# Five of eight row pairs by seven products in one up-projection block of each MLP, with the pairs in another order

## The chip, the cores and the metric

The kernel runs on one core of one Trainium2 chip. The metric is the device time of one execution in microseconds (us); three executions of the kernel before gave 1924.02, 1923.25 and 1924.7 us, so the median is 1924.02 us. The engines are named as in the profile: PE is the matmul engine (PEld its weight load), DVE the vector engine, ACT the scalar engine, POOL and SP the two others; SP issues the weight loads from memory.

## The reference

Two layers work on 256 tokens of width 2048, in float32. Layer 0 mixes tokens by a convolution module, layer 1 by latent attention. Each layer ends with the MLP that the change touches:

```python
def sq_relu_mlp(h, w1, w2):
    return jnp.square(jax.nn.relu(h @ w1)) @ w2
# per layer: x = x + mixer(rms_norm(x));  x = x + sq_relu_mlp(rms_norm(x), w1, w2)
# h: 256 x 2048, w1: 2048 x 8192, w2: 8192 x 2048
```

## The kernel before

**Float32 in three matmuls.** Every operand is split into a high part (rounded to the matmul's format, by an ACT copy) and a low part (the rest, by a DVE subtraction). A product of two operands is then three matmuls: high by high, low by high, high by low (`mm3`, lines 209 to 211). So each 1 MB piece of weights costs ACT copies and DVE subtractions before PE can use it. Pieces come through three `raw` buffers, and their parts through six `hi` and six `lo` buffers.

**The MLP's stages.** `mlp` works in two halves of the 8192 columns (`hf` 0 and 1). In a half, `UP_PLAN` lists the up-projection's blocks. Blocks 4, 5, 6 and 7 hold 512 columns each, with the weights standing in the array and the tokens moving (lines 812 and 813); results are evicted from the four `acc` banks by ACT and DVE (L829, L830, L832), squared, and split again (L715). Entries 0 and 2 are blocks of 1024 columns, with the tokens standing and the weights moving (`up_block`): these are the standing-input blocks. The order is block 4, block 5, standing-input block 0, block 6, standing-input block 2, block 7; then the down-projection of the half.

**A standing-input block.** Its 2048 input rows are eight pairs of 2 x 128 rows. For a pair, the two token tiles and the two column halves make eight products of 128x128 by 128x512, 24 matmuls (`Sums.plain`); the results gather in the four banks of the two `pair` tiles. `Sums.mixed` does the same with seven products, 21 matmuls, from sums and differences of the inputs and of the weights; it adds into the `pair` banks and into the four `acc` banks (u1, u6, u7, u5). For that, `mixed_weights` makes seven weight forms of a pair: four ACT copies, four DVE subtractions for low parts (L524, L525) and three DVE sums on `raw` (L532, L533, L534), against two copies and two subtractions of a plain pair (L176, L180). The input forms come once per half from `up_forms`, called at the (block, step) places of `UP_FORMS`; each call makes those of two pairs. `up_copies` rounds the inputs that plain pairs use. After the last seven-product pair, `Sums.parts` copies the `acc` banks out on ACT (L619) and combines them on DVE (L620 to L623).

Before, pairs 2, 3, 4 and 5 go by seven products (`UP_MIXED`), and the pairs run in the order 0, 2, 1, 3, 6, 4, 5, 7 (`UP_ORDER`) in all blocks.

**What sets the order.** The tile framework schedules the instructions of each engine in lists that are fixed when the program is built; an engine runs its list in order. In layer 0 the tables of the rotary embedding for layer 1 are made by DVE and ACT in block 5 of the second half (`beside`, small operations on `v` tiles, L1469 to L1513). Two `v` buffers serve all of this.

Of the kernel before, what the change touches and what calls it, by code (L numbers as in the profile page):

```python
# [45 lines left out]
HEAD, TAIL = (2, 1), 2  # L46
UP_PLAN, UP_ORDER, UP_MIXED = (4, 5, 0, 6, 2, 7), (0, 2, 1, 3, 6, 4, 5, 7), (2, 3, 4, 5)
UP_FORMS = ({(1, 1): 0, (1, 3): 1}, {(0, 2): 0, (1, 1): 1})
UP_COPIES = ({(1, 0): 0, (1, 2): 3}, {(1, 0): 0, (1, 2): 3})


# [31 lines left out]
def trunk_kernel(  # L83
# [59 lines left out]
    def nm(s):  # L143
        uid[0] += 1
        return f"{s}_{uid[0]}"
# [506 lines left out]
    def mlp(layer, ssq, next_gain, finish=None, before=None, beside=None, after_up=None):  # L652

        with ExitStack() as cx:
# [9 lines left out]
            def v_tile():  # L664
                rooms.clear()
                return mp.tile([P, 4, S], F32, tag="v", name=nm("v"), bufs=2)
# [10 lines left out]
                    nc.tensor.transpose(o[:, t * P : (t + 1) * P], r[:, t : t + 1].broadcast_to([P, P]), ident)  # L677
                nc.scalar.activation(r_row, o[:, :S], AF.Copy)

            def up_forms(i, fs):  # L680

                v, x = v_tile(), xt[UP_MIXED[2 * i] // 2].bitcast(F32)
                nc.vector.tensor_tensor(v, x[:, :, :S], x[:, :, S:], op=ALU.add)
                v = by_pairs(v)
                mixed_sums(*(v[:, :, j, :] for j in range(4)))
                h, l = (f[i][:, :, 3:, :] for f in fs)
                nc.scalar.activation(h, v, AF.Copy)
                nc.vector.tensor_tensor(l, v, h.bitcast(F32), op=ALU.subtract)
                x = x.rearrange("p (q k) n -> p q k n", q=2)
                for c, f in enumerate(fs):  # L690
                    nc.scalar.activation(f[i][:, :, 0, :], x[:, :, 0, c * S : c * S + P], AF.Copy)
                    nc.scalar.activation(
                        f[i][:, :, 1:3, :], x[:, :, 1, c * S : (c + 1) * S].rearrange("p q (t n) -> p q t n", t=T), AF.Copy
                    )

            def up_form(p, fs):

                i = UP_MIXED.index(p)

                def form(j):  # L700
                    return tuple(f[i // 2][:, i % 2, j, :] for f in fs)

                return form

# [27 lines left out]
            def up_block(hf, g, fs, copies):  # L732

                n = (hf * nkh + 4 * g) // 4
                sums = Sums(n, False, True)
                left = [p for p in UP_ORDER if p in UP_MIXED]

                def at_kt(c):
                    def at(k, t):
                        ts = slice(t * P, (t + 1) * P)  # L740
                        return copies[k // 4][c][:, k % 4, ts] if k // 4 in copies else (xh, xl)[c](k)[:, ts]
                    return at

                for p in UP_ORDER:
                    if p in UP_MIXED:
                        left.remove(p)
                        sums.mixed(mlp_w1[layer], 2 * p, up_form(p, fs), not left)
                        continue
                    end = p == UP_ORDER[-1]
                    if end:  # L750
                        zs = [v_tile().rearrange("p k n -> p (k n)") for _ in range(T)]
                        sums.parts(*(z[:, c * NB : (c + 1) * NB] for z in zs for c in range(2)))
                    sums.plain(mlp_w1[layer], 2 * p, at_kt(0), at_kt(1), 2 * p, end)
                for t, z in enumerate(zs):
                    o = z.rearrange("p (c n) -> p c n", c=2)
                    nc.vector.tensor_tensor(o, sums.pairs[t], o, op=ALU.add)
                    nc.scalar.activation(z, z, AF.Relu, scale=r_cols[0][:, t : t + 1])

                def turned():
                    pts = [a.rearrange("p b (k t n) -> p (b k) t n", t=T, n=P) for a in sums.pairs]  # L760
                    for c in range(2):
                        for f in range(4):
                            for t in range(T):
                                at = c * NB + f * P
                                nc.tensor.transpose(pts[c][:, f, t, :], zs[t][:, at : at + P], ident)  # L765
                    for c in range(2):
                        place(g + c)
                        v = v_tile()
                        nc.scalar.activation(v, pts[c].rearrange("p f t n -> p f (t n)"), AF.Square)
                        activations(g + c, v)  # L770

                return [turned]

            r_cols, late = [], []
            for hf in range(HALVES):
# [5 lines left out]
                fs = [[mp.tile([P, 2, 7, P], F32R, tag=f"s{c}", name=nm(f"f{c}"), bufs=N_MIXED) for _ in range(2)] for c in "hl"]  # L781
                copied = {
                    n: [mp.tile([P, 4, S], F32R, tag=f"g{c}", name=nm(f"x{c}"), bufs=ng - N_MIXED) for c in "hl"]
                    for n in UP_COPIES[hf].values()
                }
                for nth, g in enumerate(UP_PLAN):
                    if g in mixed:
                        late = up_block(hf, g, fs, {n: a for n, a in copied.items() if nth < 3 or n > 0})
                        continue
                    if nth == 0:  # L790
                        ends = [pair_tile() for _ in range(2)]
# [5 lines left out]
                    for u in range(KC // 4):  # L797
# [15 lines left out]
                                nc.tensor.matmul(ps[b][:, :S], wl[:, bs], xh(k), start=False, stop=k == KC - 1)  # L813
                        step(6)
                        if (nth, u) in UP_FORMS[hf]:
                            up_forms(UP_FORMS[hf][nth, u], fs)
                        if (nth, u) in UP_COPIES[hf]:
                            up_copies(UP_COPIES[hf][nth, u])
                        if late and u > 0:
# [1270 lines left out]
```

## Time and profile before

| what | value |
|---|---|
| median of three executions | 1924.02 us (1923.25 to 1924.7) |
| the profiled execution | 1923.38 us, its span 1921.6 us, granted PE clock 0.999 |
| PE busy | 1909.4 us (99%) |
| DVE busy | 1696.6 us (88%) |
| ACT busy | 1201.3 us (63%) |
| first standing-input block of layer 0's second half, PE | 683.01 to 723.96 us |
| the same in layer 1 | 1619.09 to 1659.90 us |

The span runs from the first to the last instruction; the execution's time has 1.8 us around it. A timeline row gives the start, the time, the engine, the line, the operation with what it writes and reads, and its count; in brackets stands the idle time before it and what ended it. Matmuls overlap, so their spacing counts and not their 0.39 us.

### The profile page before, as it was taken

How to read it: one execution, taken by the hardware profiler on the slowest of the kernel's cores; microseconds unless marked ns; L12 is line 12 of the kernel's file. 1: busy time of each engine (PE TensorE's matmuls, PEld its weight loads, DVE VectorE, ACT ScalarE, POOL GpSimd, SP SyncE). 2: the span in 40 equal slices, each digit the busy share in tenths (PEclk: the TensorE clock that was granted, in tenths of full speed). 3: DMA queues.
4: the chain of work that ended last, by engine and by line, in shares of the span. 5: the costliest groups of instructions: out<-in, count | busy, mean ns of one | idle time of the engine just before them, and what ended most of it. 6: DMA issues, size and time to landing. Idle time of an engine off the chain costs nothing.

```text
span 1921.6 us, 27587 instructions
## 1 busy us (share of the span) xinstructions
PE 1909.4 (99%) x10245; PEld 1653.2 (86%) x10245; DVE 1696.6 (88%) x2407; ACT 1201.3 (63%) x1701; POOL 248.6 (13%) x208
## 2 busy tenths in 40 slices
PE   9999999999999999999999999999999999999998
PEld 9999888888888888888888998888888888888887
DVE  7999989999999899999976765898999988898898
ACT  5667756666655666665576665576665647666554
POOL 6999200000010100000001420000000010000000
PEclk9999999999999999999999999999999999999999
DMA  7766455556585855655656445556556775655774
GB/s 228 211 185 186 156 186 196 187 186 219 176 250 198 252 167 193 229 178 199 217 168 183 138 137 177 173 176 219 188 173 225 219 246 199 219 180 195 233 221 147
DMA packets 214039, 375.43 MB, mean 195 GB/s; under 512 B 16392, under 2 KB 107792, under 8 KB 213648
## 3 DMA queue, kind: packets, MB, share of 16 engines
q1 hardware_dynamic: 208256, 363.28, 57.4%
q0 software_dynamic: 4320, 7.87, 2.2%
q10 hardware_dynamic: 1328, 2.52, 0.4%
q8 instruction: 80, 1.31, 0.3%
q14 instruction: 55, 0.45, 0.1%
HBM read 363.68 MB, written 2.10 MB: 190 GB/s over the span
## 4 chain that ended last, share of the span: by engine, by line
PE 96%; DVE 2%; ACT 1%; issue 0%; DMA 0%; DVEq 0%; ACTq 0%
PE acc L209 11%; PE acc L211 11%; PE acc L210 11%; PE pair L211 10%; PE pair L210 10%; PE pair L209 10%; PE acc L812 9%; PE acc L972 8%; PE acc L813 5%; PE pair L812 3%; PE acc L1436 2%; PE pair L813 2%; DVE sum L1059 1%; PE pair L765 1%; PE acc L1713 0%
## 5 line engine op out<-in xcount | busy, mean ns | idle before, releaser
L176 ACT ACTIVATE hi<-raw 128x1024 fp32r<-128x1024 f32 (+2 forms) x510 | 509.9, 1030 | 149.1 <-DMA raw<-in_mlp_w 44.1
L180 DVE TENSOR_TENSOR lo<-raw,hi 128x1024 fp32r<-128x1024 f32 (+2 forms) x445 | 519.2, 1193 | 89.4 <-ACT hi L176 84.7
L524 ACT ACTIVATE hi<-raw 128x1024 fp32r<-128x1024 f32 x376 | 347.0, 948 | 316.0 <-DVE raw L532 199.1
L525 DVE TENSOR_TENSOR lo<-raw,hi 128x1024 fp32r<-128x1024 f32 x376 | 400.2, 1088 | 26.9 <-ACT hi L524 21.0
L812 PE MATMUL acc<-xt,hi 128*128 128x512 f32 x768 | 268.0, 391 | 0.0
L813 PE MATMUL acc<-xt,lo 128*128 128x256 f32 x768 | 216.5, 282 | 0.0
L972 PE MATMUL acc<-xt,hi 128*128 128x256 f32 x1024 | 180.2, 281 | 0.4 <-ACT xt L1239 0.3
L611 POOL DMA_DIRECT2D xs<-v x30 | 26.3, 932 | 1128.3 <-DVE lo L180 696.2
L812 PEld LDWEIGHTS acc<-xt,hi 128*128 128x128 f32 x768 | 144.2, 188 | 30.1
L1059 DVE SCALAR_TENSOR_TENSOR sum<-ub,w_dw,sum 128x256 f32<-128x256 f32 x409 | 164.4, 485 | 3.6 <-ACT sum L1029 3.0
L180 POOL TENSOR_TENSOR lo<-raw,hi 128x1024 fp32r<-128x1024 f32 x65 | 155.0, 2408 | 18.0 <-ACT hi L176 18.0
L972 PEld LDWEIGHTS acc<-xt,hi 128*128 128x128 f32 x1024 | 154.7, 188 | 1.2 <-ACT xt L1239 0.8
L813 PEld LDWEIGHTS acc<-xt,lo 128*128 128x128 f32 x768 | 145.1, 189 | 0.3
L972 PE MATMUL acc<-xt,lo 128*128 128x256 f32 x512 | 139.2, 279 | 0.0
L532 DVE TENSOR_TENSOR raw<-raw 128x1024 f32<-128x1024 f32 x94 | 114.8, 1221 | 0.4
L209 PE MATMUL acc<-hi,sh 128*128 128x512 f32 x289 | 112.6, 390 | 0.0
L211 PE MATMUL acc<-lo,sh 128*128 128x512 f32 x289 | 112.5, 389 | 0.0
L210 PE MATMUL pair<-hi,gl 128*128 128x512 f32 (+1 forms) x264 | 101.9, 386 | 0.0
L211 PE MATMUL pair<-lo,gh 128*128 128x512 f32 (+1 forms) x264 | 101.9, 386 | 0.0
L209 PE MATMUL pair<-hi,gh 128*128 128x512 f32 (+1 forms) x264 | 101.9, 386 | 0.0
L209 PE MATMUL acc<-hi,gh 128*128 128x512 f32 x252 | 98.1, 389 | 0.0
L211 PE MATMUL acc<-lo,gh 128*128 128x512 f32 x252 | 98.0, 389 | 0.0
(381 smaller groups left out, 4299.1 us busy)
## 6 DMA issues: line engine op xcount, KB each, us to landing
raw<-in_mlp_w SPq DMA_DIRECT2D x255, 1024.0 KB, 5.5
raw<-in_conv_w_pw SPq DMA_DIRECT2D x62, 512.0 KB, 5.1
raw<-in_conv_w_pw SPq DMA_DIRECT2D x16, 1024.0 KB, 4.9
raw<-in_mla_w_o SPq DMA_DIRECT2D x16, 1024.0 KB, 5.1
raw<-in_mla_w_kv_up SPq DMA_DIRECT2D x32, 256.0 KB, 4.0
xs<-v POOLq DMA_DIRECT2D x30, 256.0 KB, 7.3
raw<-in_mla_w_in SPq DMA_DIRECT2D x8, 576.0 KB, 4.3
raw<-in_mla_w_in SPq DMA_DIRECT2D x4, 1024.0 KB
```

What stands on the lines that cost most here:

```text
L176: nc.scalar.activation(hi, raw[:, js, :], AF.Copy)
L180: eng.tensor_tensor(lo, raw, hi.bitcast(F32), op=ALU.subtract)
L209: nc.tensor.matmul(ps, sh, mh, start=start, stop=False)
L210: nc.tensor.matmul(ps, sl, mh, start=False, stop=False)
L211: nc.tensor.matmul(ps, sh, ml, start=False, stop=stop)
L524: nc.scalar.activation(hi, src, AF.Copy)
L525: nc.vector.tensor_tensor(lo, src, hi.bitcast(F32), op=ALU.subtract)
L532: nc.vector.tensor_tensor(top, raw[:, :, NB:], top, op=ALU.subtract)
L812: nc.tensor.matmul(ps[b], wh[:, bs], xhl(k), start=k == 0, stop=False)
L813: nc.tensor.matmul(ps[b][:, :S], wl[:, bs], xh(k), start=False, stop=k == KC - 1)
L972: nc.tensor.matmul(pss[c][b][:, :S], w[i][:, bs], (xh, xl)[j](k), start=k == i + j == 0, stop=end and k == k0 + nk - 1 and (i, j) == terms ...
L1059: nc.vector.scalar_tensor_tensor(out=out, in0=ubs[c][:, w : w + S], scalar=tap(c, w), in1=base, op0=ALU.mult, op1=ALU.add)
```

## The change

In the first standing-input block of the second half of each MLP, so twice in the whole run, pair 6 goes by seven products as well, and the pairs run in the order 2, 0, 3, 4, 1, 5, 6, 7. In the place before, block 5 of that half, a third call of `up_forms` makes the input forms of pair 6 alone (half of the tile, `slice(0, 1)`). All other blocks are as before.

```diff
+UP_MORE, UP_MORE_AT, UP_MORE_ORDER = 6, {1: (1, 2)}, (2, 0, 3, 4, 1, 5, 6, 7)
...
-            def up_forms(i, fs):
-
-                v, x = v_tile(), xt[UP_MIXED[2 * i] // 2].bitcast(F32)
-                nc.vector.tensor_tensor(v, x[:, :, :S], x[:, :, S:], op=ALU.add)
-                v = by_pairs(v)
+            def up_forms(n, f2, qs=slice(0, 2)):
+
+                ks = slice(2 * qs.start, 2 * qs.stop)
+                v, x = v_tile(), xt[n].bitcast(F32)
+                nc.vector.tensor_tensor(v[:, ks], x[:, ks, :S], x[:, ks, S:], op=ALU.add)
+                v = by_pairs(v)[:, qs]
                 mixed_sums(*(v[:, :, j, :] for j in range(4)))
...
-                left = [p for p in UP_ORDER if p in UP_MIXED]
+                more = UP_MORE // 2 in fs
+                order, by_seven = (UP_MORE_ORDER, (*UP_MIXED, UP_MORE)) if more else (UP_ORDER, UP_MIXED)
+                left = [p for p in order if p in by_seven]
...
-                for p in UP_ORDER:
-                    if p in UP_MIXED:
+                for p in order:
+                    if p in by_seven:
                         left.remove(p)
                         sums.mixed(mlp_w1[layer], 2 * p, up_form(p, fs), not left)
                         continue
-                    end = p == UP_ORDER[-1]
+                    end = p == order[-1]
...
+                more = {UP_MORE // 2: form_tiles()} if hf in UP_MORE_AT else {}
...
                     if g in mixed:
-                        late = up_block(hf, g, fs, {n: a for n, a in copied.items() if nth < 3 or n > 0})
+                        late = up_block(hf, g, fs | more, {n: a for n, a in copied.items() if nth < 3 or n > 0})
+                        more = {}
                         continue
...
                         if (nth, u) in UP_FORMS[hf]:
-                            up_forms(UP_FORMS[hf][nth, u], fs)
+                            n = UP_MIXED[2 * UP_FORMS[hf][nth, u]] // 2
+                            up_forms(n, fs[n])
+                        if (nth, u) == UP_MORE_AT.get(hf):
+                            up_forms(UP_MORE // 2, more[UP_MORE // 2], slice(0, 1))
```

Eight lines are added ahead of it, so that L830 of before is L838 of the change, L524 is L525, and so on.

**PE at the block's first use of the `acc` banks, layer 0.** Names with `pair` and `acc` are banks; `hi` and `lo` are weight parts, `fh`, `fl` input forms of a seven-product pair, `xh`, `xl` plain inputs. Before, the first seven-product pair follows pair 0, whose last row stands at the top:

```order
L211 MATMUL pair_7056<-lo_7068,xh_6623 128x512
L209 MATMUL acc_7057<-hi_7097,fh_6619 128x512 [waits DVE_49]
L210 MATMUL acc_7057<-hi_7097,fl_6621 128x512
L211 MATMUL acc_7057<-lo_7098,fh_6619 128x512
L209 MATMUL pair_7055<-hi_7097,fh_6619 128x512
```

Now, the block's first matmuls follow block 5's last one at the top:

```order
L818 MATMUL acc_6825<-xt_99,lo_6987 128x256
L210 MATMUL pair_7069<-hi_7077,fh_6619 128x512 [waits Activation_49]
L211 MATMUL pair_7069<-hi_7077,fl_6620 128x512
L212 MATMUL pair_7069<-lo_7078,fh_6619 128x512 [waits DVE_49]
L210 MATMUL pair_7069<-hi_7081,fh_6619 128x512 [waits Activation_49]
L211 MATMUL pair_7069<-hi_7081,fl_6620 128x512
L212 MATMUL pair_7069<-lo_7082,fh_6619 128x512 [waits DVE_49]
L210 MATMUL acc_7071<-hi_7077,fh_6619 128x512 [waits DVE_49]
```

The `acc` bank that block 5 filled is taken again after 6 matmuls instead of after 24; the DVE wait of that row is for its eviction. In layer 1 it is taken after 2.

**DVE at that eviction, layer 0.** Rows of L1486 and L1494 belong to the rotary tables. Before:

```order
L525 TENSOR_TENSOR lo_7109<-raw_7095,hi_7108 128x1024 [waits PE_49,Activation_49]
L1486 SCALAR_TENSOR_TENSOR v_7008<-v_7008 128x64 [waits DVE_49]
L830 TENSOR_TENSOR v_7042<-acc_6820,v_7042 128x256 [waits Activation_49]
L1486 SCALAR_TENSOR_TENSOR v_7008<-v_7008 128x64 [waits DVE_49]
L830 TENSOR_TENSOR v_7042<-acc_6821,v_7042 128x256 [waits Activation_49]
```

Now:

```order
L526 TENSOR_TENSOR lo_7089<-raw_7075,hi_7088 128x1024 [waits PE_49,Activation_49]
L1494 SCALAR_TENSOR_TENSOR v_7022<-v_7022 128x64 [waits DVE_49]
L526 TENSOR_TENSOR lo_7093<-raw_7075,hi_7092 128x1024 [waits PE_49,Activation_49]
L1494 SCALAR_TENSOR_TENSOR v_7022<-v_7022 128x64 [waits DVE_49]
L181 TENSOR_TENSOR lo_7120<-raw_7117,hi_7119 128x1024 [waits DMAHW0_49,PE_49,Activation_49]
L1494 SCALAR_TENSOR_TENSOR v_7022<-v_7022 128x64 [waits DVE_49]
L838 TENSOR_TENSOR v_7056<-acc_6822,v_7056 128x256 [waits Activation_49]
```

The first eviction stood behind both subtractions of pair 0 and three of pair 2's four; now it stands behind all four of pair 2's and one of pair 0's.

**ACT at the last seven-product pair, layer 0.** `hi_7291` to `hi_7306` are pair 5's weight forms of before, `hi_7313` to `hi_7328` pair 6's of the change; `hi_7343` and `hi_7365` are the first half of pair 7. Before:

```order
L524 ACTIVATE hi_7295<-raw_7289 128x512 [waits PE_49,Activation_49]
L524 ACTIVATE hi_7302<-raw_7289 128x1024 [waits DVE_49,PE_49,Activation_49]
L524 ACTIVATE hi_7306<-raw_7289 128x1024 [waits DVE_49,PE_49,Activation_49]
L176 ACTIVATE hi_7343<-raw_7341 128x1024 [waits DMAHW6_49,PE_49,Activation_49]
L619 ACTIVATE v_7331<-acc_7057 128x512 [waits PE_49]
```

Now:

```order
L525 ACTIVATE hi_7317<-raw_7311 128x512 [waits PE_49,Activation_49]
L620 ACTIVATE v_7353<-acc_7071 128x512 [waits PE_49]
L525 ACTIVATE hi_7324<-raw_7311 128x1024 [waits DVE_49,Activation_49]
L525 ACTIVATE hi_7328<-raw_7311 128x1024 [waits DVE_49,Activation_49]
L177 ACTIVATE hi_7365<-raw_7363 128x1024 [waits DMAHW6_49,Activation_49]
```

The copy of the bank u1, which waits for PE's products of this same pair, moved ahead of two of the pair's weight copies.

More of the change, by code (lines that the diff above doesn't have):

```diff
@@ L780, in mlp @@
                 gs = {}
-                fs = [[mp.tile([P, 2, 7, P], F32R, tag=f"s{c}", name=nm(f"f{c}"), bufs=N_MIXED) for _ in range(2)] for c in "hl"]
+                form_tiles = lambda: [mp.tile([P, 2, 7, P], F32R, tag=f"s{c}", name=nm(f"f{c}"), bufs=N_MIXED) for c in "hl"]
+                fs = {p // 2: form_tiles() for p in UP_MIXED[::2]}
+                more = {UP_MORE // 2: form_tiles()} if hf in UP_MORE_AT else {}
                 copied = {
```

13 lines of the change are left out of this document (6 added, 7 removed).

## The prediction

> **What bounds the kernel now.** I read the page's busy times and chain of waits first, then PE's, DVE's and ACT's timelines around the two blocks that change.
>
> ```profile
> PE 1909.4 (99%) x10245; PEld 1653.2 (86%) x10245; DVE 1696.6 (88%) x2407; ACT 1201.3 (63%) x1701; POOL 248.6 (13%) x208
> PE 96%; DVE 2%; ACT 1%; issue 0%; DMA 0%; DVEq 0%; ACTq 0%
> ```
>
> PE sets the end, so a matmul less is time less, as long as PE's inputs come in time. The 88% of DVE is a mean; what counts is the block itself. PE in layer 0's block (its first matmul, first seven-product pair, second plain pair, pair 7, a late matmul, the next block):
>
> ```profile
> 683.01 0.39 PE L209 MATMUL pair<-hi,xh 128*128 128x512 f32 x1
> 688.46 0.39 PE L209 MATMUL acc<-hi,fh 128*128 128x512 f32 x1
> 693.22 0.39 PE L209 MATMUL pair<-hi,xh 128*128 128x512 f32 x1
> 718.38 0.39 PE L209 MATMUL pair<-hi,xh 128*128 128x512 f32 x1
> 719.52 0.50 PE L211 MATMUL pair<-lo,xh 128*128 128x512 f32 x1
> 723.96 0.40 PE L812 MATMUL acc<-xt,hi 128*128 128x512 f32 x1
> PEld pair L211 <- DVE lo L180: 0.3, 1, 0.3
> ```
>
> A plain pair lasts 688.46 - 683.01 = 5.45 us, a seven-product pair 693.22 - 688.46 = 4.76, so a matmul costs 0.227 us (not the 0.39 of its row). The row at 719.52 lasts 0.50 for 0.39, and the wait's row says why: a low part of pair 7 came late. DVE reaches the end of this block with no lead left. Its work for pairs 3 and 6 and the block's tail:
>
> ```profile
> 693.34 1.82 DVE L525 TENSOR_TENSOR lo<-raw,hi 128x1024 fp32r<-128x1024 f32 x2
> 695.08 1.22 DVE L532 TENSOR_TENSOR raw<-raw 128x1024 f32<-128x1024 f32 x1
> 697.66 2.50 DVE L525 TENSOR_TENSOR lo<-raw,hi 128x1024 fp32r<-128x1024 f32 x2
> 700.08 2.35 DVE L180 TENSOR_TENSOR lo<-raw,hi 128x1024 fp32r<-128x1024 f32 x2
> 702.35 1.82 DVE L525 TENSOR_TENSOR lo<-raw,hi 128x1024 fp32r<-128x1024 f32 x2
> 715.86 1.23 DVE L525 TENSOR_TENSOR lo<-raw,hi 128x1024 fp32r<-128x1024 f32 x1 [1.21 <-ACT hi L524]
> 717.00 3.60 DVE L180 TENSOR_TENSOR lo<-raw,hi 128x1024 fp32r<-128x1024 f32 x3
> ```
>
> A seven-product pair takes DVE 700.08 - 693.34 = 6.74 us, a plain one 2.27. Per seven-product pair DVE is 1.98 us slower than PE, and per plain pair 3.18 faster. Before, four and four: DVE 36.0, PE 40.8 us. Now five and three: DVE 40.5, PE 40.2. The lead inside the block is gone, and the evictions of block 5 come on top.
>
> **What is saved.** In each of the two blocks 24 matmuls become 21: 3 x 0.227 = 0.68 us, 1.36 in all. No load is added: pair 6's 1 MB piece is fetched either way.
>
> **What is added ahead of the block.** Input forms of pair 6: on DVE an addition and a subtraction of 512 and four sums of 128; on ACT copies of 512, two of 256 and two of 128. The nearest rows in layer 0:
>
> ```profile
> L691 ACT ACTIVATE fh<-xt x1: 402/402/402, 651.2 to 651.2; 128x256 fp32r<-128x256 f32 x1
> L692 ACT ACTIVATE fh<-xt x1: 616/616/616, 651.5 to 651.5; 128x512 fp32r<-128x512 f32 x1
> 671.27 1.22 DVE L688 TENSOR_TENSOR fl<-v,fh 128x1024 fp32r<-128x1024 f32 x1
> 675.64 1.22 DVE L180 TENSOR_TENSOR lo<-raw,hi 128x1024 fp32r<-128x1024 f32 x1
> 678.11 1.22 DVE L525 TENSOR_TENSOR lo<-raw,hi 128x1024 fp32r<-128x1024 f32 x1
> 681.25 0.22 DVE L1486 SCALAR_TENSOR_TENSOR v<-v 128x64 f32<-128x64 f32 x1
> 681.39 0.69 DVE L533 TENSOR_TENSOR raw<-raw 128x512 f32<-128x512 f32 x1
> 684.66 0.42 DVE L830 TENSOR_TENSOR v<-acc,v 128x256 f32<-128x256 f32 x1
> 685.13 0.42 DVE L830 TENSOR_TENSOR v<-acc,v 128x256 f32<-128x256 f32 x1
> ```
>
> An operation of 512 holds DVE 0.6 us (0.69 less an overlap of some 0.09); one of 128 lies between the 64-wide and the 256-wide row, 0.22 and 0.42 with their tails, 0.14 and 0.33 without. Together 2 x 0.6 + 4 x (0.14 to 0.33) = 1.8 to 2.5 us of DVE. Woven between the rotary rows, each of which waits for the one before, some of it costs nothing; I take 1.3, with 0.9 and 2.5 as ends.
>
> **The first stop, layer 0.** The block now begins with pair 2, and after 6 matmuls, at 683.01 + 6 x 0.227 = 684.37, PE wants the first `acc` bank, which block 5 has just filled. Before, pair 0 filled the `pair` banks first, and the bank was wanted only at 688.46; its eviction (684.66) was hidden by that pair. Where is the eviction now? Pair 0's two subtractions (675.64 to 678.11, 2.47 us) move behind pair 2's; one of them and pair 2's last subtraction now stand ahead of the eviction, each 1.14 with a rotary row of 0.13 (681.25 to 681.39 is 0.14): 684.66 - 2.47 + 2.54 + 1.3 = 686.0. It ends 0.42 later, so PE stops from 684.37 to 686.45: **2.1 us** (1.7 to 3.3). The other three banks follow 0.47 apart, and PE takes one per 0.68.
>
> **The later stops, layer 0.** PE's first two pairs end at 683.01 + 4.76 + 5.45 + 2.1 = 695.3. On DVE four evictions (1.9), the scaling L832 and the other half of pair 0 (2.5 with rotary rows) end at 690.4; pair 3 with L715 (1.14) inside takes till 698.5, pair 4 till 705.2, pair 1 till 707.5, pair 5 till 714.2, pair 6 till 721.0. ACT's high parts follow within a pair:
>
> ```profile
> 696.39 1.07 ACT L524 ACTIVATE hi<-raw 128x1024 fp32r<-128x1024 f32 x1 [2.94 <-DVE raw L532]
> 697.84 1.06 ACT L524 ACTIVATE hi<-raw 128x1024 fp32r<-128x1024 f32 x1 [0.38 <-DVE raw L534]
> 716.68 0.58 ACT L619 ACTIVATE v<-acc 128x512 f32<-128x512 f32 x1
> ```
>
> They end 4.1 and 5.6 us after DVE began the pair (693.34). PE wants the first 9 matmuls into a pair (2.04), the second 4 later (0.9).
> - Pair 3: PE 695.3 to 700.1, no stop.
> - Pair 4: wanted 702.1, there at 702.6; then wanted 703.5, there at 704.1. **1.1 us**; it ends 705.9.
> - Pair 1 to 711.4, pair 5 to 716.2, no stop.
> - Pair 6: ACT must first copy u1, the output of this pair's first product: 716.2 + 0.7 + 0.2 = 717.1, plus 0.5; so the weight copy ends at 718.7, wanted 718.2. **0.5 us**; it ends 721.4.
> - Pair 7: the low part of its second half needs 721.0 + 2 x 1.2 and ACT's two u copies (0.6 more), 724.0; wanted 10 matmuls in, 723.7. **0.3 us**; the block ends at 727.2.
>
> Against 723.96 that is +3.2: stops 4.0, less 0.68 saved, less the 0.1 of the stop at 719.52 that it replaces.
>
> **Layer 1.** No rotary rows here.
>
> ```profile
> 1619.09 0.39 PE L209 MATMUL pair<-hi,xh 128*128 128x512 f32 x1
> 1659.90 0.40 PE L812 MATMUL acc<-xt,hi 128*128 128x512 f32 x1
> 1609.51 3.50 DVE L180 TENSOR_TENSOR lo<-raw,hi 128x1024 fp32r<-128x1024 f32 x3 [1.62 <-ACT hi L176]
> 1612.92 1.22 DVE L525 TENSOR_TENSOR lo<-raw,hi 128x1024 fp32r<-128x1024 f32 x1
> 1618.72 1.09 DVE L830 TENSOR_TENSOR v<-acc,v 128x256 f32<-128x256 f32 x3
> ```
>
> DVE waited 1.62 us for ACT; ACT's new copies (0.52 + 2 x 0.31 + 2 x 0.2, about 1.6) lengthen that, so block 5's last subtraction starts near 1611.1 and pair 2's at 1612.25. Those end at 1619.0, one of pair 0 at 1620.1, the first eviction 1620.5. PE wants that bank after 2 matmuls, 1619.54: **1.0 us** (0.5 to 1.8). From there DVE's 6.74 per seven-product pair brings pair 6's low parts at 1652.9, wanted 1653.0, and pair 7's at 1657.1, wanted 1657.1: 0 to 0.7, I take **0.3**. Net +0.7 with rounding, 1.3 - 0.68.
>
> **The sum.** +3.2 and +0.7: +3.9 us. The span goes from 1921.6 to 1925.5, the profiled execution (1.8 around it) to 1927.3; the median of the runs lies 0.64 above that execution, so it becomes 1924.02 + 3.9 = **1927.9 us**, 0.2% slower.
>
> **The rivals.**
> - *DVE's lead is enough; not slower.* If pair 6's forms slip into waits and the eviction ends by 684.4, the order is harmless and the saving remains: 1924.0 - 1.36 = 1922.7, up to 1924.5 with stops of under 2 us. For it: DVE waits 1.62 us ahead of the block in layer 1. Against: the late row at 719.52, and 2.1 us to make up. Chance 0.2.
> - *Only the first stops.* If a seven-product pair costs DVE 6.4 (four of 1.14 and three of 0.6 with no wait between dependent rows) the later stops go: 2.1 + 1.0 - 1.36 - 0.1 = +1.6, 1925.6. Against: 6.74 in the quoted pair. Chance 0.12.
> - *A longer stop, and PE's clock falls.* At the upper end of the new DVE work the first stop is 3.3 us, 1.2 more.
>
> ```profile
> 1900.00:1921.00 21.00, 13.83 (x73) 11.76 (x71) 12.98 (x34) 5.36 (x12) 0.00 (x0) 0.95 0.28 101
> 953.00:983.00 30.00, 28.78 (x145) 24.15 (x144) 27.34 (x40) 17.61 (x31) 0.00 (x0) 1.00 0.46 142
> ```
>
> In the first stretch PE stood 7.2 us and its granted clock was 0.95, so 1.05 us of 21 were lost; in the second it stood 1.2 us and the clock stayed at 1.00. With such a loss: 3.9 + 1.2 + 1.05, 1930.2. The Trainium skill (TensorE: Matmul & The Clock Gate, What's actually happening) says the clock halves after an idle window of about 3.4 us; by that rule my 2.1 us cost no clock, and both rows agree. Chance 0.08.
>
> **How the numbers follow.** My forecast has 0.6, with its own range 1926.0 to 1929.6. A change within 0.2% (3.85 us) can't be told from none here, and 3.9 stands on that edge: half of the 0.6 is within it and half slower. With the clock's 0.08, slower has 0.38 to 0.4; within 0.2% has 0.3 + 0.12 + nearly all of the 0.2, less some spread: 0.57; faster by over 0.2% is beyond the whole saving, 0.03. The range of 8 in 10 is 1923.2 to 1930.4.
>
> **What would show it.** A wait of PE on L838 near 684 of about 2 us and near 1619.5 of about 1; waits on L525 in pair 4 and pair 6 in layer 0; the block 44.2 us long in layer 0 and 41.5 in layer 1, for 40.95 and 40.81. I am wrong if PE shows no wait on an eviction, or if the time is under 1924.

## The result and the profile after

The changed kernel took 1929.5 us as the median of seven executions (1928.36 to 1931.48), against 1924.02 before (seven executions, 1923.12 to 1924.7): a ratio of 1.0029, 95% interval 1.002 to 1.0039. So it is slower by 5.5 us, where the prediction said 3.9. The traced execution of the change took 1930.75 us, span 1929.0, so it lies in the upper part of the seven; the traces differ by 7.4 us.

The page of the changed kernel, its busy times and its chain of waits; then three rows of the table of what PE waited for (in all, times, longest):

```profile
PE 1909.6 (99%) x10239; PEld 1649.5 (86%) x10239; DVE 1707.6 (89%) x2429; ACT 1205.7 (63%) x1715; POOL 248.8 (13%) x208
PE 93%; DVE 4%; ACT 1%; issue 1%; DMA 1%; SPq 0%; DVEq 0%; ACTq 0%
```

```profile
PE acc L210 <- DVE v L838: 5.0, 2, 3.7
PE acc L212 <- DVE lo L526: 0.4, 1, 0.4
PE acc L210 <- ACT hi L525: 0.3, 1, 0.3
```

PE issues six matmuls fewer (10239 for 10245), as planned; two waits for an eviction (L838) are new. In the chain DVE has 4% for 2%. PE's timeline around the two blocks:

```profile
682.26 0.39 PE L210 MATMUL pair<-hi,fh 128*128 128x512 f32 x1
...
687.45 0.50 PE L210 MATMUL acc<-hi,fh 128*128 128x512 f32 x1 [3.65 <-DVE v L838]
...
689.09 0.63 PE L212 MATMUL acc<-lo,fh 128*128 128x512 f32 x1
689.52 0.63 PE L210 MATMUL acc<-hi,fh 128*128 128x512 f32 x1
689.95 0.63 PE L211 MATMUL acc<-hi,fl 128*128 128x512 f32 x1
...
692.58 0.39 PE L210 MATMUL pair<-hi,xh 128*128 128x512 f32 x1
...
720.24 0.50 PE L210 MATMUL acc<-hi,fh 128*128 128x512 f32 x1 [0.28 <-ACT hi L525]
...
728.92 0.40 PE L817 MATMUL acc<-xt,hi 128*128 128x512 f32 x1
...
1624.28 0.39 PE L210 MATMUL pair<-hi,fh 128*128 128x512 f32 x1
1626.22 0.50 PE L210 MATMUL acc<-hi,fh 128*128 128x512 f32 x1 [1.32 <-DVE v L838]
...
1658.92 0.50 PE L212 MATMUL acc<-lo,fh 128*128 128x512 f32 x1 [0.42 <-DVE lo L526]
...
1666.83 0.40 PE L817 MATMUL acc<-xt,hi 128*128 128x512 f32 x1
```

Layer 0's block is now 728.92 - 682.26 = 46.66 us long, for 40.95; layer 1's 1666.83 - 1624.28 = 42.55, for 40.81. Together +7.45, and the span grew by 7.4. (Elsewhere small shifts cancel: PE reaches the first block 0.75 us sooner, and the rest takes 0.7 longer.)

The first pair shows how. Six matmuls end at 682.26 + 6 x 0.227 = 683.62; the next begins at 687.45, so PE stood **3.83 us**. From 688 to 692 the matmuls are 0.43 us apart in place of 0.227. The first pair takes 692.58 - 682.26 = 10.32 us instead of 4.76: 5.56 lost, 3.83 by the stop and some 1.7 by the slow matmuls. The rest of the block lost 0.94 by late weights, 0.68 was saved, and 0.11 of lateness was there before: 5.56 + 0.94 - 0.68 - 0.11 = 5.71. In layer 1 two matmuls fit ahead: 1626.22 - 1624.28 - 0.45 = 1.49 us of stop, 0.11 right behind it, no slow matmuls, 0.80 later.

Busy time and granted clock in stretches of layer 0's block (span of the row, busy PE, PEld, DVE, ACT, POOL, granted clock, DMA share, GB/s):

```profile
682.00:688.00 6.00, 2.35 (x11) 1.65 (x10) 6.00 (x15) 5.62 (x9) 0.00 (x0) 1.00 0.31 85
688.00:692.00 4.00, 4.00 (x12) 3.13 (x11) 4.00 (x9) 2.70 (x4) 0.00 (x0) 0.57 0.50 207
692.00:729.00 37.00, 36.73 (x161) 29.41 (x160) 35.29 (x40) 23.13 (x30) 0.00 (x0) 1.00 0.57 188
```

The clock fell to 0.57 behind the stop. DVE is busy 6.00 of 6.00, then 4.00 of 4.00, then 35.29 of 37; its two waits in that last stretch, 0.68 us at 720.22 and 0.61 at 724.33, are for ACT's copies. So two readings of the loss are open: **the stop reading** (the new order meets the eviction, PE stands, the clock falls; DVE's load inside the block matters little) and **the chain reading** (DVE works with hardly a pause up to the block's last low part, and PE would have to wait for it somewhere, wherever the first stop falls).

### The profile page after: what moved, and what is told of

Same layout as the page of the kernel before. It is cut to its first block, busy times and chain, and to the rows that moved or that the text cites. A ratio compares the mean times of both kernels' runs of the same rounds, so it can differ in the third digit from the quotient of the medians.

```text
span 1929.0 us, 27619 instructions
## 1 busy us (share of the span) xinstructions
PE 1909.6 (99%) x10239; PEld 1649.5 (86%) x10239; DVE 1707.6 (89%) x2429; ACT 1205.7 (63%) x1715; POOL 248.8 (13%) x208
## 4 chain that ended last, share of the span: by engine, by line
PE 93%; DVE 4%; ACT 1%; issue 1%; DMA 1%; SPq 0%; DVEq 0%; ACTq 0%
PE acc L210 11%; PE acc L212 11%; PE acc L211 11%; PE pair L212 10%; PE pair L210 10%; PE pair L211 10%; PE acc L817 8%; PE acc L980 8%; PE acc L818 4%; PE pair L817 3%; PE acc L1444 2%; PE pair L818 1%; DVE sum L1067 1%; PE pair L767 1%; DVE lo L526 0%
## 5 line engine op out<-in xcount | busy, mean ns | idle before, releaser
L181 DVE TENSOR_TENSOR lo<-raw,hi 128x1024 fp32r<-128x1024 f32 (+2 forms) x441 | 513.8, 1191 | 89.0 <-ACT hi L177 84.0
L525 ACT ACTIVATE hi<-raw 128x1024 fp32r<-128x1024 f32 (+1 forms) x384 | 353.7, 947 | 317.4 <-DVE raw L533 205.0
L526 DVE TENSOR_TENSOR lo<-raw,hi 128x1024 fp32r<-128x1024 f32 (+1 forms) x384 | 408.3, 1087 | 27.0 <-ACT hi L525 19.7
```

The source lines that it names most:

```text
L181: eng.tensor_tensor(lo, raw, hi.bitcast(F32), op=ALU.subtract)
L525: nc.scalar.activation(hi, src, AF.Copy)
L526: nc.vector.tensor_tensor(lo, src, hi.bitcast(F32), op=ALU.subtract)
```

## The experiments

Edits are against the changed kernel. Block lengths are read from each run's timeline of PE, from the block's first matmul to the next block's.

| run | layer 0, us | layer 1, us | median, us | ratio to before, 95% |
|---|---|---|---|---|
| before | 40.95 | 40.81 | 1924.02 | |
| the change | 46.66 | 42.55 | 1929.5 | 1.0029 (1.002 to 1.0039) |
| order_alone | 46.08 | 42.32 | 1928.7 | 1.0025 (1.0015 to 1.0035) |
| order_bare | 43.51 | 41.04 | 1926.67 | 1.0015 (1.0005 to 1.0025) |
| forms_only | 43.44 | 40.81 | 1925.07 | 1.0007 (0.9998 to 1.0017) |
| fill_stop | 47.36 | 42.36 | 1931.49 | 1.0037 (1.0024 to 1.005) |
| fill_order | 44.36 | 45.12 | 1929.85 | 1.0028 (1.0017 to 1.0039) |
| plain_first | 45.56 | 43.52 | 1930.1 | 1.0032 (1.002 to 1.0044) |
| l1_only | 41.63 | 42.41 | 1925.42 | 1.001 (1.000 to 1.002) |
| rope_last | 43.78 | 42.79 | 1930.76 | 1.0037 (1.0023 to 1.005) |
| rope_early | 48.31 | 43.49 | 1935.94 | 1.0062 (1.0047 to 1.0077) |
| forms_early | 49.47 | 48.1 | 1938.31 | 1.0072 (1.0055 to 1.0088) |
| pool_01 | 51.0 | 45.9 | 1938.84 | 1.0077 (1.006 to 1.0093) |

(Lengths with one decimal are counted from the end of block 5's last matmul, since the block's own first one waited.)

### The order without the fifth pair

```diff
-UP_MORE, UP_MORE_AT, UP_MORE_ORDER = 6, {1: (1, 2)}, (2, 0, 3, 4, 1, 5, 6, 7)
+UP_MORE, UP_MORE_AT, UP_MORE_ORDER = 6, {1: (1, 2)}, (2, 0, 3, 1, 6, 4, 5, 7)
...
-                order, by_seven = (UP_MORE_ORDER, (*UP_MIXED, UP_MORE)) if more else (UP_ORDER, UP_MIXED)
+                order, by_seven = (UP_MORE_ORDER, UP_MIXED) if more else (UP_ORDER, UP_MIXED)
```

Pair 6 goes plainly; its forms are still made, and nobody reads them.

> The new order's beginning without the fifth pair: four pairs by seven products in the order 2, 0, 3, 1, 6, 4, 5, 7; the input forms of pair 6 are still made, but not used. So DVE has 4.5 us less in each block than in the change, and the eviction stands where the change has it. Theory A: the first stop is as in the change (3.8 us and 1.6), with the fall of the clock in layer 0: median 1928 to 1931. Theory B: the first stop is there, but the late stops go, since DVE catches up; blocks of 43 to 45 and 41.5 to 42.5 us, median 1926 to 1929. If the fifth pair is the whole cause: no more than 1925.

Order and forms without the fifth pair cost nearly all: 46.08 and 42.32 us, 1928.7 (1929.5 for the whole change). The stop and the slow clock are there, and nothing is late after them:

```profile
687.31 0.56 PE L210 MATMUL acc<-hi,fh 128*128 128x512 f32 x1 [3.38 <-DVE v L838]
```

```profile
688.00:692.00 4.00, 4.00 (x13) 3.08 (x13) 4.00 (x9) 2.70 (x4) 0.00 (x0) 0.62 0.45 185
692.00:729.00 37.00, 37.00 (x165) 30.68 (x164) 33.69 (x37) 23.01 (x29) 0.00 (x0) 1.00 0.63 215
```

PE is busy 37.00 of 37 behind the stop, and DVE has 3.3 us to spare. With four pairs the stop reading holds. The fifth pair adds just 0.58 and 0.23 us to the blocks: in layer 0 its own saving of 0.68 is eaten by 0.94 of late weights, and a little more.

### The order and the forms, each by itself

For order_bare the call that makes pair 6's forms is left out of order_alone as well. For forms_only the forms are made and not read, and pairs and order are those of before.

```diff
 # order_bare, on top of order_alone
-                more = {UP_MORE // 2: form_tiles()} if hf in UP_MORE_AT else {}
+                more = {UP_MORE // 2: None} if hf in UP_MORE_AT else {}
...
-                        if (nth, u) == UP_MORE_AT.get(hf):
+                        if False:
 # forms_only
-UP_MORE, UP_MORE_AT, UP_MORE_ORDER = 6, {1: (1, 2)}, (2, 0, 3, 4, 1, 5, 6, 7)
+UP_MORE, UP_MORE_AT, UP_MORE_ORDER = 6, {1: (1, 2)}, (0, 2, 1, 3, 6, 4, 5, 7)
...
-                order, by_seven = (UP_MORE_ORDER, (*UP_MIXED, UP_MORE)) if more else (UP_ORDER, UP_MIXED)
+                order, by_seven = (UP_MORE_ORDER, UP_MIXED) if more else (UP_ORDER, UP_MIXED)
```

> Four pairs by seven products as before, in the new kind of order (a seven-product pair first: 2, 0, 3, 1, 6, 4, 5, 7), and no input forms of pair 6 at all. Against the run of the order alone it leaves out only the making of the unused forms. If those forms' place on DVE is what makes the first stop long (some 2 us of DVE work put in ahead of the eviction of L838), the stop of layer 0 falls from 3.8 to 1.6-2.2 us, the clock stays at 1.00, the block of layer 0 is 42.5-43.2 us long and that of layer 1 40.9-41.2, and the time is 1925.8-1926.5. If the order is enough for the stop and the forms lie in time that nobody waits for, the stop stays over 3 us, the clock falls again, the blocks stay near 46 and 42.3 and the time near 1928.7.

> The order of before (0, 2, 1, 3, 6, 4, 5, 7) and four pairs by seven products; the new input forms of pair 6 are made where the change makes them, but nothing reads them. If DVE's lead in a block that begins with a plain pair hides them (DVE 36.0 us of work against PE's 40.8 in the block), no wait appears, the blocks stay at 40.9-41.2 and the time at 1923.7-1924.4. If two microseconds of DVE work there cost as such, the block of layer 0 is 42-43 us long and the time 1925-1926.

In layer 0 the traced blocks grew by about the same: 43.51 (+2.56) for the order, 43.44 (+2.49) for the forms; together (order_alone) +5.13. In layer 1 the order costs 0.23, the forms nothing, and both together 1.51. PE's rows of order_bare, then of forms_only:

```profile
682.26 0.39 PE L210 MATMUL pair<-hi,fh 128*128 128x512 f32 x1
685.06 0.50 PE L210 MATMUL acc<-hi,fh 128*128 128x512 f32 x1 [2.40 <-DVE v L838]
```

```profile
717.74 0.50 PE L210 MATMUL pair<-hi,fh 128*128 128x512 f32 x1 [0.58 <-ACT hi L525]
719.00 0.51 PE L212 MATMUL pair<-lo,fh 128*128 128x512 f32 x1 [0.53 <-DVE lo L526]
725.99 0.40 PE L817 MATMUL acc<-xt,hi 128*128 128x512 f32 x1
```

Without the forms PE gets the first bank 2.4 us sooner (685.06 for 687.45): 0.84 of it because DVE started sooner in this execution (the row that waits for the stores, shown further down for the change, starts at 645.03 and not 645.87), the other 1.5 are what the forms take of DVE. The clock stayed at full. But here the program's list puts one matmul and not six ahead of the first `acc` bank, so PE still stands 685.06 - 682.49 = 2.57 us. (The traced execution is the fastest of this run's ten, 1924.99 us of up to 1930.84, so these blocks need not be those of the median.)

forms_only went against what I expected of it. DVE work that nothing reads, in the old order and with an eviction that nobody waits for, made weights late in pairs 5 and 7 of layer 0. The block began 0.46 us sooner than before and ended 2.03 later, 725.99 for 723.96: DVE was 0.58 later already ahead of the forms (L715 at 669.61 for 669.03), and the forms, with the places that the lists gave the rest of DVE's work, add the other 1.45. So even before, DVE reached the end of that block with nothing in hand, and in layer 1 it had this much to spare. This speaks for the chain reading. (The times of the runs rose by only 1.1 us, an amount that a measurement here hardly tells from none.)

### The stop filled with useless matmuls

32 transposes into a bank that is overwritten later stand behind the first six matmuls in layer 0's block; they add no result.

```diff
...
+            elif self.fill:
+                work = [work[i] for i in (4, 5, 0, 1, 2, 6, 3)]
-            for ps, i, (wh, wl) in work:
+            for at, (ps, i, (wh, wl)) in enumerate(work):
+                if self.fill and at == 2:
+                    for r in range(self.fill):
+                        nc.tensor.transpose(self.e[1][1][:, r % 4 * P : (r % 4 + 1) * P], ident, ident)
+                    self.fill = 0
...
+                sums.fill = 32 if more and layer == 0 else 0
```

> The changed kernel, with 32 transposes of 128 columns (3.5 us) put into PE's queue in layer 0's block between the products into the pair banks and the first product into an acc bank, so that PE works through most of its stop; their results are overwritten. Nothing else moves. Theory A (the loss is PE's first stop and the fall of its clock after it): the clock stays at 1.00 after the stop, the twelve matmuls at 0.43 us go back to 0.227, and the block is 1.7 us shorter than 46.7, the median near 1927.8. Theory B (DVE works without a pause from block 5 to the block's last low part, and its end sets the block's end): the clock stays up too, but the time is the same within 0.5 us (1929.0 to 1929.9); PE waits longer for weight parts in pairs 4, 6 and 7 instead.

> The run of the order alone (four pairs, unused forms made, stop of 3.8 us and slow clock in layer 0) with 32 transposes of no use in that stop, to keep TensorE busy. Here DVE has no fifth pair to work on. If the slower matmuls behind the stop are a loss by themselves where DVE isn't the bound, the block of layer 0 falls from 46.1 to 44.2-44.5 us, the clock row there stays at 1.00, and the time is 1926.7-1927.3. If DVE's chain sets the end here as well, the block stays at 45.7-46.3 with new waits on the low parts or high parts of weights (L526, L525) behind the start, and the time at 1928.3-1929.

In layer 0's block the clock stayed at full in both. Row of the stretch for fill_stop and its new waits, then the row for fill_order:

```profile
688.00:692.00 4.00, 4.00 (x19) 3.31 (x18) 4.00 (x9) 2.07 (x4) 0.00 (x0) 1.00 0.48 196
```

```profile
PE acc L212 <- DVE lo L526: 1.3, 3, 0.6
PE pair L210 <- ACT hi L525: 0.6, 1, 0.6
PE pair L212 <- DVE lo L526: 0.5, 1, 0.5
```

```profile
688.00:692.00 4.00, 4.00 (x19) 3.30 (x18) 4.00 (x11) 2.07 (x3) 0.00 (x0) 1.00 0.56 224
```

With four pairs the block of layer 0 became 1.72 us shorter (44.36 for 46.08): there the slow clock cost what its matmuls show. With five pairs it didn't become shorter at all (47.36 for 46.66): PE came to the later pairs sooner and waited there for DVE's low parts and ACT's high parts. Some of this is the fill's own doing, since DVE's list changed with it. In pair 4 L535 now stands behind two of the pair's subtractions, and DVE then waits for ACT, which it does not in the change:

```profile
704.05 0.69 DVE L535 TENSOR_TENSOR raw<-raw 128x512 f32<-128x512 f32 x1
705.94 1.23 DVE L526 TENSOR_TENSOR lo<-raw,hi 128x1024 fp32r<-128x1024 f32 x1 [1.21 <-ACT hi L525]
```

DVE was 0.17 us ahead of the change before this and 0.98 behind it after (it begins pair 1 at 707.08 for 706.10), so some 1.15 of the 47.36 us belong to the list. Without them the block would have been about 46.2 us long, an estimate: 0.5 shorter than in the change, and not the 1.7 of the slow clock. **With five pairs the chain sets the end, with four the stop and the clock.** In the whole change both are nearly equal, so that taking one away gains little.

The time of fill_order nevertheless didn't fall, since layer 1's block, where nothing was filled, came out 2.8 us longer than in order_alone. Its rows in fill_order, with the DVE row that waits for the residual's stores some 40 us ahead of the block, and that row in order_alone:

```profile
1584.70 1.23 DVE L691 TENSOR_TENSOR v<-xt 128x1024 f32<-128x1024 f32 x1 [3.54 <-DMA xs<-v]
...
1625.00 0.76 PE L210 MATMUL acc<-hi,fh 128*128 128x512 f32 x1 [2.43 <-DVE v L845]
```

```profile
1586.01 1.23 DVE L685 TENSOR_TENSOR v<-xt 128x1024 f32<-128x1024 f32 x1 [3.05 <-DMA xs<-v]
```

In fill_order that row starts 37.24 us ahead of the block, in order_alone 38.68 (block starts 1621.94 and 1624.69). DVE's work from there to the first eviction is the same, so the stop grew from 1.39 to 2.61 us, and the clock fell there too. So the length of the stop hangs on when the two `v` buffers come free of stores, long before the block, as much as on when PE arrives.

### A plain pair first

```diff
-UP_MORE, UP_MORE_AT, UP_MORE_ORDER = 6, {1: (1, 2)}, (2, 0, 3, 4, 1, 5, 6, 7)
+UP_MORE, UP_MORE_AT, UP_MORE_ORDER = 6, {1: (1, 2)}, (0, 2, 3, 1, 4, 5, 6, 7)
```

> Five pairs by seven products as in the change, but the block begins with the plain pair 0 (order 0, 2, 3, 1, 4, 5, 6, 7), so the acc banks are wanted 5.4 us later. Theory A: no wait on an eviction and no fall of the clock; the late stops of 1.5 us in layer 0 and 0.8 in layer 1 stay, so blocks of about 41.7 and 41.0 us, median 1924 to 1926. Theory B: DVE has the same work, so the waits move to the later seven-product pairs; blocks of 45 to 46.5 and 42 to 43 us, median 1928 to 1930.

No wait on an eviction, full clock, and yet 45.56 and 43.52 us. What PE waited for in this run:

```profile
PE acc L210 <- ACT hi L525: 2.9, 3, 1.5
PE acc L212 <- DVE lo L526: 1.9, 3, 0.7
```

The stops moved into the later pairs: layer 0's block is 1.1 us shorter than in the change, layer 1's 1.0 longer. So the first stop is not what makes five pairs dear; another order of the same work doesn't help.

### One layer alone, and the change a second time

```diff
-                more = {UP_MORE // 2: form_tiles()} if hf in UP_MORE_AT else {}
+                more = {UP_MORE // 2: form_tiles()} if hf in UP_MORE_AT and layer == 1 else {}
...
-                        if (nth, u) == UP_MORE_AT.get(hf):
+                        if layer == 1 and (nth, u) == UP_MORE_AT.get(hf):
```

> The change in layer 1's block alone; layer 0's block is as before. If each block's loss is its own, layer 0 is 40.9-41.1 us long, layer 1 42.3-43.1 (42.55 and 43.04 in two executions of the change), and the time is 1925.3-1926.2. If DVE reaches layer 1's block at a time that doesn't depend on how late PE is, PE comes 5.7 us sooner and stops longer at the first acc bank there (2.6 us or more, the clock falls as in the filled run of the order): block 44.5-46 us, time 1927.5-1929.

> The change as it is, a second profiled execution. If the stops are set by the lists of the engines alone, the first stop in layer 0 is again 3.6-4.0 us with the slow clock behind it and the blocks are 46.4-46.9 and 42.3-42.8 us long. If they hang on when data arrive in this execution (DVE's wait for the stores of the residual near 645 us, 3.05 us before and 3.47 in the change), they differ by a microsecond or more.

Layer 1 alone: 42.41 us there and 1925.42 in all, as the first reading had it. Layer 0's block, with the lists of before, was 41.63, not 40.95: pairs 5 and 7 were 0.3 and 0.2 late, a sign again of how little DVE has in hand there. DVE's list in this block is that of before, row for row; it started 0.19 us later (645.26 for 645.07), and the block ended 0.21 later (724.17 for 723.96), although PE had begun it 0.47 sooner. So even with the lists of before the end of this block follows DVE, not PE. The change a second time gave 46.42 and 43.04 us, a first stop of 3.56 again with the slow clock behind it, and in layer 1 a stop of 1.96 for 1.49; its one time was 1931.11. The lists set the picture, and half a microsecond hangs on the execution.

### DVE's work moved elsewhere

Three runs move work out of the busy stretch, one gives some of it to POOL.

```diff
 # rope_last: the rotary tables at the end of block 7
-                    if beside is not None and hf == nth == 1:
+                    if beside is not None and hf == 1 and nth == 5:
 # rope_early: inside block 4
+                        if beside is not None and (hf, nth, u) == (1, 0, 1):
+                            beside(v_tile())
+                            beside = None
...
-                    if beside is not None and hf == nth == 1:
-                        beside(v_tile())
-                        beside = None
 # forms_early: pair 6's forms at the last step of block 4
-UP_MORE, UP_MORE_AT, UP_MORE_ORDER = 6, {1: (1, 2)}, (2, 0, 3, 4, 1, 5, 6, 7)
+UP_MORE, UP_MORE_AT, UP_MORE_ORDER = 6, {1: (0, 3)}, (2, 0, 3, 4, 1, 5, 6, 7)
 # pool_01: low parts of the plain pairs 0 and 1 of the block on POOL
-        def plain(self, w, k, hi, lo, k0, end, middle=None):
+        def plain(self, w, k, hi, lo, k0, end, middle=None, eng=None):
...
-            at_j = split(load([rows(w, k, 2, self.n * NB, 2 * NB)], 2), nc.vector)
+            at_j = split(load([rows(w, k, 2, self.n * NB, 2 * NB)], 2), nc.vector if eng is None else eng)
...
-                    sums.plain(mlp_w1[layer], 2 * p, at_kt(0), at_kt(1), 2 * p, end)
+                    sums.plain(mlp_w1[layer], 2 * p, at_kt(0), at_kt(1), 2 * p, end, eng=nc.gpsimd if more and p in (0, 1) else None)
```

> The change whole, but layer 0's rotary tables (some 4.4 us of small DVE rows, 3.5 of them ahead of the eviction) are made at the end of block 7 and the start of the down-projection instead of block 5. By the unbroken DVE work from 662 us on: the block of layer 0 loses 4.0-4.4 us of it and comes to 42.3-42.8 us, as layer 1's 42.55 without tables; by the first stop and the clock: stop 0.3 instead of 3.8, no slow clock, 41.3-41.8. Layer 1 stays at 42.3-42.8. Where the tables go DVE is 98% busy, but PE has no wait there (100%), so that 0 to 4 us of the gain may be given back: time 1925.3-1929.5. If it isn't the tables that make layer 0 worse than layer 1, the block stays over 45.

> The change whole, but the rotary tables (L1477 to L1494 on DVE, 20-odd small rows, some 3.6 us of them ahead of the eviction and 1 us behind) are made in the block but one before, where DVE has idle time (15 of 22 us busy between 640 and 662). Both theories want layer 0 to come to the size of layer 1, which has no tables: first stop 0.2-1.6 us instead of 3.8, clock at 1.00, block of layer 0 41.5-42.7 us instead of 46.7, layer 1 as it was (42.4-42.7), time 1924.8-1926. If it was not the tables that made layer 0 worse than layer 1, but a late arrival of data or the eviction's own place, the stop stays over 2.5 us and the time over 1927.5.

> The change whole, but the input forms of pair 6 are made one block earlier, at the last step of block 4 (between 652 and 662 us), where DVE waits three times for ACT (0.55, 0.55 and 1.79 us idle), instead of in block 5. That takes some 2.0 us out of the stretch from 662 us on in which DVE has no idle time. If the block's end in layer 0 is set by the length of that stretch, the block becomes 44.2-44.9 us long for 46.66; if by the first stop and the slow clock behind it, the stop becomes 1.6-2.0 us, the clock stays at 1.00 and the block is 42.6-43.2. In layer 1 (42.55) both want 41-42.5. Times: 1926.3-1927.2 by the first, 1924.7-1925.6 by the second. If ACT's copies for the forms delay the high parts that DVE waits for there, or the v buffer is still held by the residual's stores, nothing is won: 1929 or more.

> The changed kernel, with the low parts of the plain pairs 0 and 1 of the two blocks made by POOL instead of DVE: four subtractions of 1.14 us less on DVE in each block, 2.4 us each on POOL, which is idle there. Theory A: the eviction comes 1.1 us earlier, so the first stop in layer 0 falls from 3.8 to 2.7 us, perhaps without the fall of the clock: median 1926.5 to 1928.4. Theory B: DVE's chain is 4.5 us shorter in each block, so layer 0's block goes from 46.7 to about 42 us and layer 1's from 42.5 to 40.2 to 41: median 1923 to 1925.

**rope_last** shortened layer 0's block to 43.78, by 2.9 us for 4.4 us of rows taken out, and fell between what the two readings wanted. The tables had covered a wait of the new forms, which now stands open, as it does in layer 1:

```profile
675.23 0.69 DVE L690 TENSOR_TENSOR fl<-v,fh 128x512 fp32r<-128x512 f32 x1 [1.35 <-ACT fh L689]
685.68 0.50 PE L210 MATMUL acc<-hi,fh 128*128 128x512 f32 x1 [2.55 <-DVE v L838]
```

The lists of this run put 2 matmuls and not 6 ahead of that bank, which is 0.9 us more of stop: the eviction begins 1.8 us sooner than in the change (685.20 for 686.98), and the stop is only 1.1 us shorter. The time didn't fall (1930.76): the traced execution came to layer 1's block only 0.66 us sooner, not 2.64. Part of the rest is seen where the tables went: from 815 to 850 us DVE is busy 34.8 of 35 us, and between 815 and 900 PE stood 0.7 us and waited for high parts of weights (L525), which it did not in the change.

**rope_early** and **forms_early** made it worse by 6 to 9 us. I had taken DVE's idle time in block 4 for free time. The largest piece of it (3.47 us at 645.87) is a wait for a buffer; whatever needs a `v` buffer there waits for it, and holds up all that is listed behind. DVE in rope_early, then in forms_early:

```profile
644.99 0.17 DVE L1477 CAST v<-rot 128x2 f32<-128x2 int32 x1 [3.32 <-DMA xs<-v]
652.68 1.23 DVE L685 TENSOR_TENSOR v<-xt 128x1024 f32<-128x1024 f32 x1 [2.96 <-DMA xs<-v]
```

```profile
645.58 1.22 DVE L685 TENSOR_TENSOR v<-xt 128x1024 f32<-128x1024 f32 x1 [3.45 <-DMA xs<-v]
652.00 0.69 DVE L685 TENSOR_TENSOR v<-xt 128x512 f32<-128x512 f32 x1 [1.79 <-DMA xs<-v]
688.50 0.80 PE L210 MATMUL acc<-hi,fh 128*128 128x512 f32 x1 [5.59 <-DVE v L838]
```

In both the operation that used to come first there (L685 at 645.87) or the one behind it waits for a second store. In forms_early the lists moreover put one matmul (layer 0) and none (layer 1) ahead of the first `acc` bank, so that PE stood longer still.

**pool_01** was to take 4.5 us of low parts from DVE. POOL takes 2.4 us for each, and DVE got nothing out of it. The lists moreover put no matmul ahead of the first `acc` bank in either block, 1.4 us more of stop in layer 0 by itself (6 x 0.227). DVE's rows ahead of the eviction, with POOL's row, and one of layer 1:

```profile
683.60 0.22 DVE L1494 SCALAR_TENSOR_TENSOR v<-v 128x64 f32<-128x64 f32 x1
684.59 4.88 POOL L181 TENSOR_TENSOR lo<-raw,hi 128x1024 fp32r<-128x1024 f32 x2 [36.75 <-ACT hi L177]
684.87 2.37 DVE L1494 SCALAR_TENSOR_TENSOR v<-v 128x64 f32<-128x64 f32 x1
687.16 0.41 DVE L838 TENSOR_TENSOR v<-acc,v 128x256 f32<-128x256 f32 x1
687.50 2.06 DVE L1494 SCALAR_TENSOR_TENSOR v<-v 128x64 f32<-128x64 f32 x1
...
1631.01 3.48 DVE L840 SCALAR_TENSOR_TENSOR v<-v,r_row 128x1024 f32<-128x1024 f32 x1
```

While POOL's two rows run, a DVE row of 0.22 us takes 2.37 and then 2.06, and one of 1.22 takes 3.48; the eviction between them, which reads one operand from a bank, keeps its 0.41. The Trainium skill (SBUF — State Buffer, Who interferes with whom) says that a DVE instruction with two inputs from SBUF contends with a GpSimd instruction that reads SBUF, and that the shared ports are an exclusive lock; these rows agree.

No run beat the kernel before.

## Why the prediction was right or wrong

**The direction, the places and the time** were right: 1927.9 forecast, 1929.5 measured, inside the forecast's own range of 1926.0 to 1929.6. In part this is luck. In the traces the two blocks grew by 7.45 us, nearly twice the forecast's 3.9; the traced execution, forecast at 1927.3, took 1930.75, and only because most executions of the change were shorter than that one does the median lie in the range. And by the prediction's own chances a change within 0.2% was likelier (0.57) than one slower by more (0.4), and the latter came. The waits stand where it put them but one: on L838 at both block starts, on L525 in pair 6 (720.24), and late parts in pair 7 of layer 0 (0.2 and 0.3 us on weight loads). The wait in pair 4 didn't come: PE was by then 2.7 us later than forecast (pair 4 begins at 702.81 for 700.1).

**The saving** of 0.68 us per block stands: 6 matmuls fewer, at 0.227 us where nothing is late.

**The first stop of layer 0** was the term mis-sized: 2.1 us (1.7 to 3.3) forecast, 3.83 measured. The step "684.66 - 2.47 + 2.54 + 1.3 = 686.0" gave the eviction; it came at 686.98. And PE began at 682.26, where I had kept 683.01 of before. That is 0.98 + 0.75 = 1.73, the whole miss. DVE's rows of before, then of the change:

```profile
645.07 1.23 DVE L683 TENSOR_TENSOR v<-xt 128x1024 f32<-128x1024 f32 x1 [3.05 <-DMA xs<-v]
669.03 1.23 DVE L715 TENSOR_TENSOR gl<-v,gh 128x1024 fp32r<-128x1024 f32 x1
```

```profile
645.87 1.23 DVE L685 TENSOR_TENSOR v<-xt 128x1024 f32<-128x1024 f32 x1 [3.47 <-DMA xs<-v]
670.28 1.22 DVE L715 TENSOR_TENSOR gl<-v,gh 128x1024 fp32r<-128x1024 f32 x1
686.98 0.42 DVE L838 TENSOR_TENSOR v<-acc,v 128x256 f32<-128x256 f32 x1
```

From L715 to the first eviction DVE took 16.70 us, for 15.63 before: I had it at 17.0, so the work was counted well. The step's trade of subtractions (2.47 out, 2.54 in) is borne out too: in order_bare, without the forms, the first eviction begins at 684.59, where before had 684.66. What I had held fixed moved: DVE started 0.80 us later, behind the stores, and then waited 0.44 longer for a copy of ACT's (1.79 us at 662.05 for 1.35 at 660.82), so that L715 came 1.25 later; and PE came 0.75 sooner. I took the distance between the two engines from one execution of another program as if it were a constant; in these runs it moved by up to 1.6 us in layer 0 and 1.9 in layer 1.

**The slow clock** had been a rival with a chance of 0.08, at a stop of 3.3 us. It came, at 3.83, and cost some 1.7 us against the rival's 1.05. The row of before that gave the 1.05 holds no such price: PE's last matmul in it starts at 1913.55, the granted clock stays at 1.00 until 1919.0, and no matmul runs at the lower one. So it is partly by luck that the rival's time, 1930.2, is nearer to 1929.5 than the forecast's 1927.9. The sentence that 2.1 us would cost no clock is borne out: layer 1's 1.49 cost none, nor did 2.17 in layer 1 of rope_early. But fill_stop shows that the loss of clock isn't what makes the whole change slow: without it the time was 1931.49, still over 1929.5 with the list's 1.15 us taken off.

**The later stops** were forecast at 1.9 us in layer 0 and came to 0.94. The likely reason is that PE was later there by the excess of the first stop and the slow clock: in fill_stop and plain_first, where PE isn't held up at the start, they are larger. (The prediction's line for pair 3 adds up to 698.3 and not 698.5, which takes 0.2 us off the 1.9.) That DVE has "no lead left" in this block was the right sentence, and it should have carried the sum: in forms_only the forms alone made the block's end 1.45 us later, without any change of order.

**The new DVE work** was taken at 1.3 us (0.9 to 2.5); the runs with and without the forms give 1.5.

**Layer 1**: forecast +0.7, measured +1.74: a stop of 1.49 for 1.0, inside its bounds, and later stops of 0.80 for 0.3, just above them. (Its 1.3 - 0.68 is 0.62, which it put down as 0.7.) The rivals "DVE's lead is enough" and "only the first stops" are out: the evictions are waited for, and weights are late in every run of five pairs.

What stays open: why PE came to layer 0's block 0.1 to 0.9 us sooner in all runs but before's and rope_early's, and why the stores of the residual landed up to 1.1 us later. One traced execution each, and two of the change, don't tell a property of the program from chance.

## What to carry to other kernels

Where two engines are nearly even in a block, a first wait, the slow clock behind it and a later wait are not a sum: take each away alone, and the next in line appears. Add up the work of the fuller engine from its last real pause to the block's end, and ask which wait that pause is; one that waits for a buffer is not free time for more work in that buffer. And a stop that is the difference of two engines' positions is known only as well as those positions: bound it by their scatter, not only by the work moved.

## What the runs showed of the hardware

PE's clock fell behind stops of 3.83 and 3.55 us (the change, order_alone), and also behind one of 2.61 (fill_order, layer 1), but not behind stops of 2.57 (order_bare) and 2.73 (rope_last). So between 2.61 and 2.73 us, at least, the length alone doesn't decide. The Trainium skill (TensorE: Matmul & The Clock Gate, What's actually happening) says that the window in which activity is judged runs freely, about 3.4 us long; that place in the window matters would fit these five, though no run here shows the window itself. After these three falls 8 or 9 matmuls came 0.43 us apart, then the spacing was 0.227 again: the slow stretch lasted some 3.4 us (688.25 to 691.65 in the change). After the longer stops in layer 0 of rope_early (5.1 us) and forms_early (5.7) some 11 matmuls were slow.

A store that POOL issues and that frees a `v` buffer sets DVE's start some 40 us ahead of the block (3.03 to 3.81 us of wait near 645 us in the traces). And the same table of pairs gives other lists after small edits: 0, 1, 2 or 6 matmuls stood ahead of the first `acc` bank in these kernels, and each one fewer is 0.227 us more of stop.
